# Weight sums of a seven-product matmul scheme: two by one accumulating DMA each, two on VectorE, with another order of the operands

## The chip, the cores and the metric

The kernel runs on one core of a Trainium2 chip. The metric is device time in microseconds (us), the median of several runs of the same program. The core has five engines that matter here: TensorE (PE; its weight loads are listed as PEld), VectorE (DVE), ScalarE (ACT), GpSimd (POOL) and SyncE (SP). SP issues most DMAs, POOL issues the DMAs that add to their destination while they write it.

## The reference

One step of a hybrid encoder layer for 512 prompt frames and 64 sample frames, 576 columns in all. Everything is float32.

```
h   = x @ W_in                            # combined projection for two groups of heads
mix = concat(ForgettingAttention(h_A), IndexedSparseAttention(h_B))
x   = LN1(alpha * x + mix @ W_o)
x   = LN2(alpha * x + relu(x @ W_up)^2 @ W_down)      # 1024 -> 4096 -> 1024
x   = x + sigmoid(x @ W_g + b_g) * (p @ W_ple)
```

The change touches only the line with `W_up` and `W_down`.

## The kernel before, in words

**Split weights.** TensorE multiplies in a rounded float32 format, so each weight tile is split into a high part (a cast on ACT, line 185, tile `whl` from `wraw` or `wsum`) and a low part (source minus high part on DVE, line 189), and each product is three matmuls: high times high, high times low, low times high. The activations are split in the same way.

**Groups and pairs.** `W_up` and `W_down` are cut into eight groups of 512 hidden units. Groups 0 and 1 are done directly. In groups 2 to 7 of `W_up`, and for groups 2 to 5 of `W_down`, two 128-column weight tiles form a *pair*, and the four 2 by 2 block products of a pair are made with seven products in place of eight. A pair needs seven operands, called P1, Z1, U2, P2, U3, X4, Z2. With b11, b21 the two halves of the first tile and b12, b22 those of the second, the program's sources are: P1 = b11, P2 = b21, Z2 = b22, and four sums: Z1 = b12 + b11, U3 = b12 + b22, U2 = b11 + b12 + b22, X4 = U2 + b21. There are 20 pairs: 12 of `W_up` and 8 of `W_down`, in the order 4 up, 4 down, 4 up, 4 down, 4 up.

**How a pair is loaded.** `Weights.load` takes two of four raw slots (`wraw`) as soon as every split of the pair that held them has been put into the program. SP loads the two tiles (line 159). `sum_loads` makes the sums in a tile `wsum` of two halves, t0 and t1 (two such tiles exist): SP loads b12 into t0 (line 221) and b11 into t1 (line 222); POOL adds b22 to t0 (line 223), adds b11 to the first half of the second raw tile, which is then Z1 (line 224), and adds t0 to t1, which is then U2 (line 225). Line 209, the function `total`, makes X4 on DVE from t1 and b21, into b11's place.

**What sets the order.** Each operand has a number `h`, in the order in which TensorE uses it (in `W_up` pairs that of `range(7)`, in `W_down` pairs that of the list `D_SEQ`, which goes by names). The two split instructions and `total` wait in a list sorted by a key near `h`. `drive` steps the main generator; one step (tick) is six matmuls, a product of a pair has 12 matmuls, so a pair of `W_up` is 14 ticks. At each tick `WT.step(2)` puts up to two pieces into the program, the first of the list only, and only if its due time (`when`, in ticks after the load) has come and if the ring of split tiles (`hl_ring`, nine in this stage) has room: `h - oldest < len(hl_ring)`. `WT.half` forces what is still missing when a product needs it. The framework then places the instructions on the engines by its own time estimates; the order in the program is the priority, not always the order on an engine. Each engine works its own list strictly in that order.

**Evacuation.** In `up_sums`, P1, U2 and U3 accumulate one after the other in one bank of a PSUM tile, P2 goes to its other bank, Z1 and Z2 accumulate in a second tile, X4 has a third. What is read between them: P1 and U2 copied to `u` by ACT (lines 1416, 1417), `r0 = P2 + u0` on DVE (line 1418), U3 copied by ACT and `r3 = Z - u0` on DVE (line 1419), then lines 1420 and 1421 for X4 and Z2. `r` and `u` are tiles of a pool; after Z2 the functions `after1` to `after3` square and split `r` (lines 1365 to 1392; lines 1375 and 1376 write the tiles `hq` and `hs`). In `down_sums` DVE adds each finished product to `Y` (line 1453). A done function is put into the program six matmuls after its product ends.

**Memory.** `WT.ring` gives split slots: six ("a"), three ("b") and, up to group 1 only, four more ("l").

Of the kernel before, what the change touches and what calls it, by code (L numbers as in the profile page):

```python
# [9 lines left out]
F32 = mybir.dt.float32  # L10
F32R = mybir.dt.float32r
AF = mybir.ActivationFunctionType
OP = mybir.AluOpType
# [19 lines left out]
HW = NT // 2  # L33
# [3 lines left out]
def tile_hybrid_step(ctx: ExitStack, tc: tile.TileContext, I, O):  # L37
    nc = tc.nc
    PE, ACT, DVE, POOL, SP = nc.tensor, nc.scalar, nc.vector, nc.gpsimd, nc.sync
# [4 lines left out]
    def f(ap):  # L44
        return ap.bitcast(F32)
# [13 lines left out]
    evq, clock = [], [0]  # L59
# [38 lines left out]
    LOADT = 4  # L98
# [16 lines left out]
    class Weights:  # L115
# [21 lines left out]
        def load(self, issue=True, force=False):  # L137

            if self.loaded == len(self.items):
                return False  # L140
            it = self.items[self.loaded]
            if len(it["aps"]) == 2 and self.sums is None:
                assert not force
                return False
            slots = sorted(self.raw_ring, key=lambda x: self.raw_own.get(x[1], -1))[:len(it["aps"])]
            for _, tag in slots:
                prev = self.raw_own.get(tag, -1)
                while prev >= 0 and self.items[prev]["left"]:
                    if not force:
                        return False  # L150
                    self.emit()
            views = []
            for (pool, tag), ap in zip(slots, it["aps"]):
                self.raw_own[tag] = self.loaded
                k, c = ap.shape[1:]
                t = pool.tile([128, 1024], F32, name="wraw", tag=tag)
                v = t[:, :k * c].rearrange("p (k c) -> p k c", k=k)
                if issue:
                    SP.dma_start(v, ap)
                views.append(v)  # L160
            if len(it["aps"]) == 2:
                self.sum_loads(views, it["aps"])
            self.raw[self.loaded] = views
            it["when"] = {h: clock[0] + LOADT * len(it["aps"]) for h in it["h"]}
            if len(it["aps"]) == 2:
                for x, n in zip((Z1, U2, U3, X4), (3, 4, 3, 4)):
                    it["when"][it["h"][x]] = clock[0] + LOADT * n
            ps = self.pieces_of(it, views)
            it["left"] = len(ps)
            for key, h, fn in ps:  # L170
                self.np += 1
                insort(self.pieces, (key, self.np, it, h, fn))
            self.loaded += 1
            return True
# [18 lines left out]
        def pieces_of(self, it, views):  # L193

            eng = POOL if it["pool"] else DVE
            k, c = views[0].shape[1:]
            if len(it["h"]) == 2:
                if k == 1:
                    cuts = [views[0][:, :, :c // 2], views[0][:, :, c // 2:]]
                else:  # L200
                    cuts = [views[0][:, :(k + 1) // 2], views[0][:, (k + 1) // 2:]]
                hs = [self.split(h, src, eng) for h, src in zip(it["h"], cuts)]
                return [(h + 1.5 * x, h, fns[x]) for h, fns in zip(it["h"], hs) for x in (0, 1)]
            b11, b21, b12, b22 = [v[:, x:x + 4] for v in views[:2] for x in (0, 4)]
            tot = views[2]
            h = it["h"]

            def total():
                DVE.tensor_tensor(b11, tot[:, 1], b21, OP.add)
            ps = [(max(h[P1] + 1.6, h[X4] - 1.4), h[X4], total)]  # L210

            for x, src in ((P1, b11), (Z1, b12), (U2, tot[:, 1]), (P2, b21), (U3, tot[:, 0]), (X4, b11), (Z2, b22)):
                high, low = self.split(h[x], src, DVE)
                ps += [(h[x], h[x], high), (h[x] + 1.5, h[x], low)]
            return ps

        def sum_loads(self, views, aps):

            t = self.sums()
            b11, b21, b12, b22 = [ap[:, x:x + 4] for ap in aps for x in (0, 4)]  # L220
            SP.dma_start(t[:, 0], b12)
            SP.dma_start(t[:, 1], b11)
            POOL.dma_start(t[:, 0], b22, accum_op=OP.add)
            POOL.dma_start(views[1][:, 0:4], b11, accum_op=OP.add)
            POOL.dma_start(t[:, 1], t[:, 0], accum_op=OP.add)
            views.append(t)

        def landed(self):
# [45 lines left out]
            return Unit([self.hv[h] for h in it["h"]], k, c)  # L274


    P1, Z1, U2, P2, U3, X4, Z2 = range(7)
    WT = Weights()

    def gemm(ps, W, kmap, aH, aL, cols, yield_every=6, first=True, last=True, wc=slice(0, 128), k0=0,  # L280
# [772 lines left out]
    for x, tag in ((0, "k32"), (1, "t2")):  # L1053
        t = sb.tile([128, NT], F32, name="praw", tag=tag)
# [33 lines left out]
    fb = ctx.enter_context(tc.tile_pool(name="fb", bufs=1))  # L1088
    psN = ctx.enter_context(tc.tile_pool(name="psN", bufs=1, space=PS))
    psB = ctx.enter_context(tc.tile_pool(name="psB", bufs=1, space=PS))  # L1090
    WT.ring(fb, 1, 3, "b")
    pS = ExitStack()
    fs = pS.enter_context(tc.tile_pool(name="fs", bufs=1))
    pL = ExitStack()
# [213 lines left out]
    def sums_of_x():  # L1308

        q = {(h, k): Y[:, 4 * k:4 * k + 4, (A, B)[h]] for h in (0, 1) for k in (0, 1)}  # L1310
        s12 = base.tile([128, 2, 2, 4, HW], F32R, name="s12", tag="AH")
        SX[1], SX[2] = [[s12[:, x, part] for part in (0, 1)] for x in (0, 1)]
        s3 = fs.tile([128, 2, 4, HW], F32R, name="s3")
        SX[3] = [s3[:, part] for part in (0, 1)]
        SX[4] = [t[:, 0:4, B] for t in (BH, BL)]
        r1, r2 = [fs.tile([128, 4, HW], F32, name="r", bufs=2) for _ in range(2)]

        def split(x, r):
            ACT.copy(SX[x][0], r)
            yield 1  # L1320
            DVE.tensor_tensor(SX[x][1], r, f(SX[x][0]), OP.subtract)
            yield 1

        DVE.tensor_tensor(r1, q[1, 0], q[1, 1], OP.subtract)
        yield 1
        yield 1
        DVE.tensor_tensor(r2, r1, q[0, 0], OP.subtract)
        yield 1
        yield from split(1, r1)
        yield from split(2, r2)  # L1330
        DVE.tensor_tensor(r1, q[0, 0], q[1, 0], OP.subtract)
        yield 1
        DVE.tensor_tensor(r2, q[0, 1], r2, OP.add)
        yield 1
        yield from split(3, r1)
        yield from split(4, r2)
# [12 lines left out]
    def up_sums(g, quarters=False):  # L1349
# [7 lines left out]
        def pair(m):  # L1357
            hs = WT.items[U["P", g, m]]["h"]

            r = fs.tile([128, 4, HW], F32, name="r", bufs=2)  # L1360
            u = fs.tile([128, 2, HW], F32, name="u")
            tt = DVE.tensor_tensor

# [49 lines left out]
            ps = {P1: G[:, 0, :HW], P2: G[:, 1, :HW], Z1: Z}  # L1413
# [19 lines left out]
        for m in range(2):  # L1433
            yield from pair(m)
# [71 lines left out]
    drive(seq(wo2(B, L1B, 0), ple()), 24, L1, 24, False)  # L1506
    drive(up(0, (L1A, L1B)), 16, L1, 16, False)
    XS = sums_of_x()
    n_xs = 11

# [163 lines left out]
```

## Time and profile before

| | |
|---|---|
| median of 3 runs | 840.4 us (839.18 to 842.44) |
| the profiled execution | 842.88 us, its span 841.2 us |
| PE busy | 799.1 us (95% of the span), 5820 matmuls |
| PEld busy | 770.3 us (92%) |
| DVE busy | 566.3 us (67%) |
| ACT busy | 478.1 us (57%) |
| POOL busy | 183.6 us (22%) |
| DMA | 107.70 MB, mean 128 GB/s |

A share is that of the whole span; a stage can look different. The stage with the pairs lies between about 440 and 735 us. "Idle before" in a row is the time the engine stood still ahead of that instruction, with what ended it behind the arrow. PEclk is the share of full speed that the clock of TensorE was granted. Buffer numbers are left out of tile names: `s` stands for the sums of x, `hs` and `hq` for those of the hidden units, `g`, `n` and `m` for PSUM tiles.

### The profile page before, as it was taken

Reading aid. Unit: us, or ns where it says so; the run is one execution under the profiler, and the core shown is the slowest. Engines: PE = TensorE matmul, PEld = TensorE weight load, DVE = VectorE, ACT = ScalarE, POOL = GpSimd, SP = SyncE. Lnnn points to the kernel's source line nnn. Section 1 sums busy time; section 2 is a strip of 40 time slices with the busy share of each in tenths; the row PEclk is TensorE's granted clock in tenths of the full one; section 3 lists DMA queues with packets and bytes.
Section 4 is the critical chain, followed back from the end, with each engine's and each line's share of the span. In section 5 each row is a group of like instructions: output and inputs, shape, how many; then the busy total and the mean of one; then the engine's idle time right before and its main releaser. Section 6 shows DMA issues by size and latency. Waiting matters only on the chain.

```text
span 841.2 us, 15352 instructions
## 1 busy us (share of the span) xinstructions
PE 799.1 (95%) x5820; PEld 770.3 (92%) x5820; DVE 566.3 (67%) x1188; ACT 478.1 (57%) x1041; POOL 183.6 (22%) x191
## 2 busy tenths in 40 slices
PE   7999899999999999999999889989889899999997
PEld 7998898899999999999999788988889799899997
DVE  5789999955458557897444567666668556567643
ACT  5578555788888544785312457335665237635451
POOL 7203435354531101200002111222112120012200
PEclk9999999999999999999999899999989999999999
DMA  8435333163213224323136757877667774741011
GB/s 283 159 59 139 93 93 107 66 199 110 85 55 104 67 97 151 135 104 126 52 74 164 161 139 175 199 173 197 160 141 190 183 184 119 261 153 51 14 38 64
DMA packets 44618, 107.70 MB, mean 128 GB/s; under 512 B 6656, under 2 KB 10496, under 8 KB 44416
## 3 DMA queue, kind: packets, MB, share of 16 engines
q1 hardware_dynamic: 35904, 90.98, 34.5%
q0 software_dynamic: 8640, 15.73, 11.7%
q8 instruction: 46, 0.75, 0.4%
q14 instruction: 28, 0.23, 0.1%
HBM read 87.36 MB, written 9.54 MB: 115 GB/s over the span
## 4 chain that ended last, share of the span: by engine, by line
PE 58%; DVE 14%; DMA 11%; issue 10%; ACT 5%; POOL 1%; SPq 0%; DVEq 0%; POOLq 0%; ACTq 0%
PE g L287 33%; PE m L287 11%; PE n L287 4%; DMA wsum<-wsum 3%; DMA wsum<-in_w_down_dram 2%; DVE dbias L655 2%; DMA wsum<-in_w_up_dram 2%; DVE m L653 2%; ACT whl L185 2%; DMA wraw<-in_w_up_dram 2%; DVE whl L189 1%; DMA wraw<-in_w_down_dram 1%; PE V L930 1%; PE T L56 1%; DVE PT L911 1%
## 5 line engine op out<-in xcount | busy, mean ns | idle before, releaser
L185 ACT CAST whl<-wraw 128x512 fp32r<-128x512 f32 (+1 forms) x234 | 140.3, 612 | 158.5 <-PE g L287 120.7
L189 DVE TENSOR_TENSOR whl<-wraw,whl 128x512 fp32r<-128x512 f32 (+1 forms) x200 | 138.6, 705 | 87.4 <-ACT whl L185 86.6
L287 PE MATMUL g<-BH,whl 128*128 128x288 f32 (+2 forms) x864 | 184.5, 299 | 0.3 <-ACT u L1419 0.2
L287 PE MATMUL m<-AH,whl 128*128 128x288 f32 x736 | 178.7, 310 | 0.0
L287 PEld LDWEIGHTS g<-BH,whl 128*128 128x128 f32 x864 | 143.1, 190 | 3.2 <-ACT u L1419 1.1
L287 PEld LDWEIGHTS m<-AH,whl 128*128 128x128 f32 x736 | 127.4, 190 | 1.1
L287 PE MATMUL g<-BL,whl 128*128 128x288 f32 (+2 forms) x432 | 128.0, 297 | 0.0
L287 PE MATMUL m<-AL,whl 128*128 128x288 f32 x368 | 109.6, 298 | 0.0
L287 PEld LDWEIGHTS g<-BL,whl 128*128 128x128 f32 x432 | 82.0, 190 | 0.1
L287 PEld LDWEIGHTS m<-AL,whl 128*128 128x128 f32 x368 | 70.1, 191 | 0.1
L862 ACT ACTIVATE sP<-sP,st 128x128 f32<-128x128 f32 (+4 forms) x72 | 39.7, 551 | 36.5 <-DVE st L854 36.2
L189 POOL TENSOR_TENSOR whl<-wraw,whl 128x512 fp32r<-128x512 f32 x34 | 44.5, 1307 | 62.5 <-ACT whl L185 50.8
L287 PE MATMUL g<-s,whl 128*128 128x288 f32 x288 | 46.5, 304 | 10.3 <-DVE r L1418 9.7
L287 PE MATMUL g<-hidE,whl 128*128 128x288 f32 (+2 forms) x384 | 52.9, 295 | 1.0 <-ACT u L1419 1.0
L287 PEld LDWEIGHTS g<-hidE,whl 128*128 128x128 f32 x384 | 51.5, 188 | 1.3 <-ACT u L1419 1.2
L287 PEld LDWEIGHTS g<-s,whl 128*128 128x128 f32 x288 | 40.3, 191 | 13.3 <-DVE r L1418 11.7
L287 PE MATMUL g<-hidO,whl 128*128 128x288 f32 (+2 forms) x384 | 52.2, 296 | 0.0
L185 ACT CAST whl<-wsum 128x512 fp32r<-128x512 f32 x40 | 24.8, 619 | 47.2 <-PE g L287 20.5
L287 PEld LDWEIGHTS g<-hidO,whl 128*128 128x128 f32 x384 | 51.4, 189 | 0.0
L287 PE MATMUL g<-hq,whl 128*128 128x288 f32 x288 | 47.2, 303 | 1.9 <-ACT u L1419 1.0
L911 DVE TENSOR_TENSOR PT<-T,PT 128x128 fp32r<-128x128 f32 (+1 forms) x64 | 31.0, 485 | 22.0 <-ACT PT L910 21.7
L287 PEld LDWEIGHTS g<-hq,whl 128*128 128x128 f32 x288 | 40.6, 190 | 4.8 <-ACT u L1419 1.4
(301 smaller groups left out, 1649.1 us busy)
## 6 DMA issues: line engine op xcount, KB each, us to landing
wraw<-in_w_up_dram SPq DMA_DIRECT2D x32, 512.0 KB, 4.4
wraw<-in_w_down_dram SPq DMA_DIRECT2D x32, 512.0 KB, 4.3
wraw<-in_w_qkv_dram SPq DMA_DIRECT2D x23, 512.0 KB, 4.1
wsum<-in_w_up_dram SPq DMA_DIRECT2D x24, 256.0 KB, 4.1
wsum<-wsum POOLq DMA_DIRECT2D x20, 256.0 KB, 4.9
wsum<-in_w_down_dram SPq DMA_DIRECT2D x16, 256.0 KB, 4.1
wraw<-in_w_gate_dram SPq DMA_DIRECT2D x8, 512.0 KB, 4.4
wraw<-in_w_o_dram SPq DMA_DIRECT2D x8, 384.0 KB, 3.1
```

What stands on the lines that cost most here:

```text
L56: PE.transpose(out, in_, ident[:n, :n])
L185: ACT.copy(self.hv[h][0], src)
L189: eng.tensor_tensor(lv, src, f(hv), OP.subtract)
L287: PE.matmul(ps, W(w, kw, wc), a[:, ka, cols], start=(first and i == 0), stop=(last and i == n - 1), skip_group_check=chain)
L653: DVE.max(m, s)
L655: DVE.match_replace(out=s, in_to_replace=m, in_values=s, imm_value=GONE)
L862: ACT.activation(j["P"], j["P"], AF.Exp, bias=j["st"][:, 0:1], scale=-1.0, accum_out=s)
L911: DVE.tensor_tensor(t[:, 1, :n, c], v, f(t[:, 0, :n, c]), OP.subtract)
L930: PE.matmul(ps[:, c], w, j["PT"][:, x, kb, c], start=(kb == 0 and x == 0), stop=(kb == i and x == 1))
```

## The change

U2 is no longer made by two more DMAs (SP's load of b11 into t1 and POOL's addition of t0 to t1) but by an addition on DVE, `t1 = t0 + b11`, a new piece in the sorted list with the key `h[U2] - 0.4`. Z1 and U3 stay as one accumulating DMA each; X4 stays on DVE. The due times become 10 ticks for P1, P2 and Z2 and 18 ticks for the four sums, where they were 8 for P1, P2 and Z2, 12 for Z1 and U3, and 16 for U2 and X4; for single tiles they stay at 4. The order of the operands in `W_up` pairs becomes P1, P2, U2, Z1, U3, X4, Z2; that of `W_down` pairs, by names, stays. The ring "b" has four split slots in place of three; the tile `r` has one buffer in place of two, and the second tile of `sums_of_x` shares the place of `hsum`.

```
-            it["when"] = {h: clock[0] + LOADT * len(it["aps"]) for h in it["h"]}
+            it["when"] = {h: clock[0] + LOADT for h in it["h"]}
             if len(it["aps"]) == 2:
-                for x, n in zip((Z1, U2, U3, X4), (3, 4, 3, 4)):
-                    it["when"][it["h"][x]] = clock[0] + LOADT * n
+                for x in range(7):
+                    it["when"][it["h"][x]] = clock[0] + (10 if x in (P1, P2, Z2) else 18)
...
-            def total():
-                DVE.tensor_tensor(b11, tot[:, 1], b21, OP.add)
-            ps = [(max(h[P1] + 1.6, h[X4] - 1.4), h[X4], total)]
+            ps = [(h[U2] - 0.4, h[U2], lambda: DVE.tensor_tensor(tot[:, 1], tot[:, 0], b11, OP.add)),
+                  (max(h[P1] + 1.6, h[X4] - 1.4), h[X4], lambda: DVE.tensor_tensor(b11, tot[:, 1], b21, OP.add))]
...
             SP.dma_start(t[:, 0], b12)
-            SP.dma_start(t[:, 1], b11)
             POOL.dma_start(t[:, 0], b22, accum_op=OP.add)
             POOL.dma_start(views[1][:, 0:4], b11, accum_op=OP.add)
-            POOL.dma_start(t[:, 1], t[:, 0], accum_op=OP.add)
...
-    P1, Z1, U2, P2, U3, X4, Z2 = range(7)
+    P1, P2, U2, Z1, U3, X4, Z2 = range(7)
...
-    WT.ring(fb, 1, 3, "b")
+    WT.ring(fb, 1, 4, "b")
...
-        r1, r2 = [fs.tile([128, 4, HW], F32, name="r", bufs=2) for _ in range(2)]
+        r1, r2 = [fs.tile([128, 4, HW], F32, name=n) for n in ("r", "hsum")]
...
-            r = fs.tile([128, 4, HW], F32, name="r", bufs=2)
+            r = fs.tile([128, 4, HW], F32, name="r")
```

## The prediction

> **What bounds the kernel now.** I read the page first, then the waits of TensorE in the stage with the pairs, then the rows around its longest waits, and last what each of those waited for.
>
> ```profile
> span 841.2 us, 15352 instructions
> PE 799.1 (95%) x5820; PEld 770.3 (92%) x5820; DVE 566.3 (67%) x1188; ACT 478.1 (57%) x1041; POOL 183.6 (22%) x191
> PEclk9999999999999999999999899999989999999999
> ...
> 440.00:735.00 295.00, 269.77 (x1866) 257.73 (x1865) 186.98 (x347) 148.93 (x284) 50.08 (x58) 0.96 0.70 174
> ...
> PE g L287 <- DVE r L1418: 9.7, 5, 4.8
> PE g L287 <- DVE Y L1453: 6.8, 4, 3.8
> PE n L287 <- DVE r L1419: 4.9, 3, 4.0
> ```
>
> TensorE is the bound, yet in the 295 us with the pairs it stands still for 25.2 us (295 less 269.77), at a clock of 0.96. The reader is to see that it never waits there for a weight's DMA: the three largest lines are all evacuations by DVE. Here are the five long ones (start, duration, idle before in brackets), and one short one:
>
> ```profile
> 475.00 0.61 PE L287 MATMUL n<-BH,whl 128*128 128x288 f32 x1 [3.98 <-DVE r L1419]
> 503.63 1.07 PE L287 MATMUL g<-s,whl 128*128 128x288 f32 x6 [3.01 <-DVE r L1418]
> 517.58 1.06 PE L287 MATMUL g<-s,whl 128*128 128x288 f32 x6 [0.88 <-DVE r L1418]
> 548.92 1.33 PE L287 MATMUL g<-hs,whl 128*128 128x288 f32 x5 [2.69 <-DVE Y L1453]
> 611.58 1.81 PE L287 MATMUL g<-s,whl 128*128 128x288 f32 x6 [4.79 <-DVE r L1418]
> 658.92 3.13 PE L287 MATMUL g<-hs,whl 128*128 128x288 f32 x12 [3.79 <-DVE Y L1453]
> ```
>
> The five make 18.26 us. Each also costs clock: the windows behind them (length; busy PE, PEld, DVE, ACT, POOL; granted clock; DMA share; GB/s), and one behind the short wait:
>
> ```profile
> 475.00:481.00 6.00, 6.00 (x25) 6.00 (x26) 4.03 (x9) 4.26 (x10) 1.44 (x2) 0.51 0.64 132
> 503.60:508.10 4.50, 4.25 (x20) 3.90 (x21) 2.60 (x5) 3.06 (x7) 0.50 (x1) 0.63 0.77 163
> 548.90:553.10 4.20, 4.18 (x20) 4.20 (x21) 2.52 (x5) 0.62 (x1) 1.42 (x2) 0.59 0.97 223
> 611.60:616.60 5.00, 4.95 (x19) 4.60 (x20) 2.55 (x5) 2.96 (x7) 0.85 (x1) 0.50 0.85 166
> 658.90:663.00 4.10, 4.08 (x21) 4.10 (x22) 2.31 (x5) 0.62 (x1) 0.98 (x2) 0.65 0.89 208
> 517.00:527.00 10.00, 8.28 (x54) 7.30 (x55) 7.39 (x17) 8.29 (x17) 0.87 (x1) 1.00 0.65 175
> ```
>
> Length times one minus clock is 2.94, 1.67, 1.72, 2.50 and 1.44 us, 10.27 in all; the wait of 0.88 us cost none. So 28.5 us hang on five moments. Why DVE was late there is in its own rows and ACT's:
>
> ```profile
> 473.89 0.69 DVE L209 TENSOR_TENSOR wraw<-wsum,wraw 128x512 f32<-128x512 f32 x1 [4.32 <-DMA wsum<-wsum]
> 546.75 0.69 DVE L209 TENSOR_TENSOR wraw<-wsum,wraw 128x512 f32<-128x512 f32 x1 [4.29 <-DMA wsum<-wsum]
> 656.75 0.69 DVE L209 TENSOR_TENSOR wraw<-wsum,wraw 128x512 f32<-128x512 f32 x1 [5.38 <-DMA wsum<-wsum]
> 501.26 1.14 ACT L185 CAST whl<-wraw 128x512 fp32r<-128x512 f32 x2 [3.35 <-DMA wraw<-in_w_down_dram]
> 609.22 1.14 ACT L185 CAST whl<-wraw 128x512 fp32r<-128x512 f32 x2 [5.13 <-DMA wraw<-in_w_down_dram]
> ```
>
> In three, `total` (line 209) stood at the head of DVE's list until line 225's DMA had landed, with the evacuation behind it. In two, ACT stood at a cast whose source line 224 adds to, and DVE behind ACT.
>
> **The change part by part.** *The chain of U2.* The DMAs of POOL around these moments, and two rows of the page (KB each, median us to landing):
>
> ```profile
> 468.36 0.85 POOL L225 DMA_DIRECT2D wsum<-wsum  x1 [5.11 <-DMA wsum<-in_w_up_dram]
> 495.57 0.86 POOL L225 DMA_DIRECT2D wsum<-wsum  x1 [6.20 <-DMA wraw<-in_w_down_dram]
> 496.20 1.10 POOL L224 DMA_DIRECT2D wraw<-in_w_down_dram  x1
> 602.92 1.14 POOL L224 DMA_DIRECT2D wraw<-in_w_down_dram  x1
> ...
> wsum<-wsum POOLq DMA_DIRECT2D x20, 256.0 KB, 4.9
> wsum<-in_w_up_dram POOLq DMA_DIRECT2D x12, 256.0 KB, 5.1
> ```
>
> Line 225 goes out when t0 has landed, so at 468.36 both inputs of the new DVE addition were there, 5.5 us before `total` could start at 473.89. Two additions of 0.69 us end at about 469.8; the wait of 4.32 us is gone, and so are, by the same reckoning (4.9 us median against 4.29 and 5.38), the other two to within half a microsecond. Term A: 3.98 + 2.69 + 3.79 = 10.46 us of standing still, and their clock, 2.94 + 1.72 + 1.44 = 6.10. What is late next there is t0 itself, which the next term but one prices.
>
> *The addition for Z1.* Line 224 stands behind line 225 on POOL (496.20 behind 495.57) and now goes out right behind line 223. It took 501.26 less 496.20 = 5.06 us and 609.22 less 602.92 = 6.30 us, with line 225's bytes moving beside it. Line 222 and 225 move 256 KB each; at the stage's 174 GB/s 256 KB are 1.5 us. I take 0.6 us earlier issue and 1.5 us from lighter traffic, and for the longer one 1 us more: of 3.01 and 4.79 us, 0.9 and 1.7 remain. Term B: 5.2 us. For the clock I take all of 1.67 and half of 2.50, 2.9 us, as the remaining waits are near the 0.88 that cost none. The bounds: nothing saved (both raw tiles land no sooner, and their landing released line 225) and all, 7.80 + 4.17.
>
> [...]
>
> *The added DVE work.* Twenty additions of 0.69 us are 13.8 us on an engine busy 187 of 295 us; by themselves they lie beside TensorE's work. Their danger is the wait for t0, at the head of DVE's list. The nearest rows are line 225's, which show when t0 had landed, and the cast of U2 of the same pair:
>
> ```profile
> 475.47 0.85 POOL L225 DMA_DIRECT2D wsum<-wsum  x1 [4.61 <-DMA wsum<-in_w_up_dram]
> 483.77 0.62 ACT L185 CAST whl<-wsum 128x512 fp32r<-128x512 f32 x1 [0.76 <-PE g L287]
> ```
>
> The cast came 8.3 us after t0 and waited for a free slot, not for data. If the addition stands just ahead of its cast, it waits for nothing; if it is placed as early as its inputs allow, it can wait. Bounds: 0, and what `total` costs TensorE now, 10.46 us. I take 2.0, nearer to the row of no wait.
>
> *The order and the single `r`.* P2 is now second, so line 1418 comes two products sooner, just behind the last reads of the previous pair's `r`:
>
> ```profile
> 492.30 0.46 DVE L1421 TENSOR_TENSOR r<-n,u 128x288 f32<-128x288 f32 x1 [0.25 <-PE n L287]
> 495.41 0.75 DVE L1376 TENSOR_TENSOR hq<-r,hq 128x576 fp32r<-128x576 f32 x1
> 494.88 1.81 PE L287 MATMUL g<-s,whl 128*128 128x288 f32 x12
> ```
>
> `r` is free at 496.16 and line 1418 (0.45 us) done at 496.6. A product takes some 1.6 us (12 matmuls, pipelined), so P1, P2 and the first half of U2 end 4.0 us after Z2 at 492.1, at 496.1; the second half waits for line 1418, as the row at 503.63 shows for U3 now: 0.5 us at each of the six places where a `W_up` pair that feeds `hq` follows another, 3.0 us. Bounds: 0 (PE takes other matmuls first) and two splits of 0.69 us queued ahead, 1.9 x 6 = 11. Z1, now fourth, gains 3.2 us of slack, worth nothing where it isn't late; in `W_down`, where it was, the order stays.
>
> *Due times, ring, memory.* A pair's load goes out some 14 ticks before the ring has room for its P1 and 18 before U2, so 10 and 18 hardly bind: nothing. One more slot lets splits run one product (1.6 us) further ahead; since both load and split move, nothing. SP loses 20 issues, POOL 20 of 0.86 us and their waits; neither is waited for otherwise. `hsum` in `sums_of_x` is free before its first pair: nothing.
>
> *New places.* Every engine's order is laid anew. I add one new wait of the smallest kind that costs clock: 2.69 + 1.72 = 4.4 us, between none and two.
>
> *Sum:* 10.46 + 6.10 + 5.2 + 2.9 - 2.0 - 3.0 - 4.4 = 15.3 us less. The profiled execution took 842.88 us (1.68 outside the span), 2.48 above the median of 840.4; the changed one's would be 827.6, the median 825.1. I predict 825.
>
> **The rivals.**
>
> *The new addition blocks DVE (slower).* DVE works its list in order, and the addition needs no free slot, only t0 and b11; placed as early as its inputs seem ready, it stands there for w us in each of 20 pairs. TensorE paid 10.46 us for 13.99 us of `total`'s three long waits, 0.75 for one, so 15w. Without the 2.0 the gains are 17.3 us; it decides from w = 1.2 us. At 1.7 us the cost is 25.5 and the time 840.4 - 17.3 + 25.5 = about 849. For it: three of `total`'s waits were over 4 us, so the order on DVE does count on DMAs sooner than they land. Against it: the chain ahead is one DMA shorter, and the cast at 483.77. Chance 0.15.
>
> *Eaten at the pair boundaries (no change).* Term B saves nothing, line 1418 costs its upper 11.2: 10.46 + 6.10 - 2.0 - 11.2 - 4.4 = 1 us less, 839. For it: DVE's and ACT's work behind Z2 is densest there. Chance 0.13.
>
> *The DMAs for Z1 stay late.* Only A: 16.56 - 2.0 - 3.0 - 4.4 = 7.2 less, 833. For it: at 495.57 the raw tile's landing was the release. Chance 0.10.
>
> *All five vanish and nothing new comes:* 28.5 less, 812. For it: waits this short have one cause each. Chance 0.12.
>
> *The due times do nothing* (above) is part of my forecast.
>
> The forecast has the other 0.50, with 816 to 832 as its own range (the addition, the order and new waits at 0; or one wait more and the addition at twice its price). A change under 0.5% (4.2 us) can hardly be told from none. Faster: 0.50 + 0.10 + 0.12 = 0.72; same 0.13; slower 0.15. The range 812 to 843 leaves out the slower rival and little else.
>
> **What would show it.** Right: line 209's additions no longer waiting for `wsum` over 2 us, at most one row of PE with over 2 us of idle time between 440 and 735, a clock of 0.98 to 0.99 there, a DMA share of about 0.6, and 17 us of PE's idle time (25.2 - 10.46 - 5.2 + 2.0 + 3.0 + 2.69). Wrong: DVE waiting for `wsum` at the new addition in most pairs (first rival); PE waiting for line 1418 or 1416 behind each Z2 (second); ACT still at `wraw` near the first `W_down` pair (third); or a wait in a stage before 440, where I expect no change.

## The result and the profile after

The changed kernel takes 835.02 us (median of 8 runs, 832.27 to 836.41) against 842.1 for the kernel before, run beside it: a ratio of 0.9909, interval 0.9883 to 0.9934. It is faster by 7 us. The forecast was 15.3 us.

Line numbers behind 209 are three lower now: `total` is still line 209, the new addition on DVE line 208, POOL's addition of b22 to t0 line 221 and that for Z1 line 222, the matmul line 284, the copies of P1 and U2 lines 1413 and 1414, `r0` line 1415, `r3` line 1416, the addition to `Y` line 1450.

First the page of the changed kernel:

```profile
span 834.7 us, 15261 instructions
PE 794.7 (95%) x5820; PEld 765.5 (92%) x5820; DVE 577.4 (69%) x1208; ACT 478.1 (57%) x1041; POOL 166.8 (20%) x171
PEclk9999999999999999999999999999999999999999
```

No slice shows a lower clock any more. Now the same stage of 295 us as before, and four stretches behind waits of TensorE (columns as in the prediction):

```profile
440.00:735.00 295.00, 272.33 (x1920) 259.58 (x1919) 201.00 (x373) 154.29 (x293) 30.90 (x36) 0.98 0.52 136
540.00:545.00 5.00, 4.71 (x24) 4.71 (x25) 3.55 (x7) 0.62 (x1) 0.00 (x0) 0.67 0.29 67
571.00:577.00 6.00, 5.70 (x31) 5.70 (x32) 1.79 (x4) 1.82 (x4) 0.88 (x2) 0.72 0.69 179
649.00:654.00 5.00, 4.73 (x34) 4.55 (x35) 3.44 (x7) 0.62 (x1) 0.00 (x0) 1.00 0.18 56
664.00:669.00 5.00, 5.00 (x26) 5.00 (x27) 3.16 (x6) 0.62 (x1) 0.00 (x0) 0.66 0.14 52
```

The clock rose from 0.96 to 0.98, but TensorE still stands still for 22.7 us (295 less 272.33; 25.2 before). In the waits of that stage line 209 has no wait for a DMA any more; the addition ahead of it has (total, times, longest):

```profile
DVE wsum L208 <- DMA wsum<-in_w_up_dram: 23.5, 8, 4.5
...
PE g L284 <- DVE Y L1450: 7.5, 5, 2.7
...
PE g L284 <- ACT u L1413: 6.0, 4, 2.3
...
PE g L284 <- DVE r L1415: 5.3, 3, 2.4
DVE wsum L208 <- DMA wraw<-in_w_up_dram: 4.8, 2, 3.4
```

The two lines of L208 are 28.3 us in ten pairs. Two pairs stand before 440, and one of `W_down` waited 0.9 us: over the whole run DVE stood at the new addition for 35.6 us in 13 of the 20 pairs, among them all twelve of `W_up`, which is 1.8 us for a pair on average. And these are the rows: PE's with over 1.4 us of idle time ahead of them, and the waiting additions on DVE that stand before them.

```profile
470.58 0.68 DVE L209 TENSOR_TENSOR wraw<-wsum,wraw 128x512 f32<-128x512 f32 x1
474.08 0.69 DVE L208 TENSOR_TENSOR wsum<-wsum,wraw 128x512 f32<-128x512 f32 x1 [2.81 <-DMA wsum<-in_w_up_dram]
477.79 1.06 PE L284 MATMUL g<-s,whl 128*128 128x288 f32 x6 [2.34 <-ACT u L1413]
507.91 1.06 PE L284 MATMUL g<-s,whl 128*128 128x288 f32 x6 [1.48 <-DVE r L1415]
538.82 0.69 DVE L208 TENSOR_TENSOR wsum<-wsum,wraw 128x512 f32<-128x512 f32 x1 [2.69 <-DMA wsum<-in_w_up_dram]
540.29 2.14 PE L284 MATMUL g<-hs,whl 128*128 128x288 f32 x12 [1.76 <-DVE Y L1450]
559.62 0.84 POOL L221 DMA_DIRECT2D wsum<-in_w_up_dram  x1 [10.44 <-DMA wsum<-in_w_up_dram]
566.70 0.69 DVE L208 TENSOR_TENSOR wsum<-wsum,wraw 128x512 f32<-128x512 f32 x1 [4.27 <-DMA wsum<-in_w_up_dram]
570.80 0.45 DVE L1415 TENSOR_TENSOR r<-g,u 128x288 f32<-128x288 f32 x1
571.30 1.06 PE L284 MATMUL g<-s,whl 128*128 128x288 f32 x6 [2.37 <-DVE r L1415]
616.05 1.06 PE L284 MATMUL g<-s,whl 128*128 128x288 f32 x6 [1.48 <-DVE r L1415]
647.79 0.69 DVE L208 TENSOR_TENSOR wsum<-wsum,wraw 128x512 f32<-128x512 f32 x1 [3.54 <-DMA wsum<-in_w_up_dram]
649.27 1.86 PE L284 MATMUL g<-hs,whl 128*128 128x288 f32 x12 [2.60 <-DVE Y L1450]
662.43 0.69 DVE L208 TENSOR_TENSOR wsum<-wsum,wraw 128x512 f32<-128x512 f32 x1 [3.43 <-DMA wraw<-in_w_up_dram]
664.00 2.77 PE L284 MATMUL g<-hs,whl 128*128 128x288 f32 x12 [2.72 <-DVE Y L1450]
689.15 0.69 DVE L208 TENSOR_TENSOR wsum<-wsum,wraw 128x512 f32<-128x512 f32 x1 [2.52 <-DMA wsum<-in_w_up_dram]
692.35 0.40 PE L284 MATMUL g<-BH,whl 128*128 128x288 f32 x1 [2.08 <-ACT u L1413]
```

Read one moment: at 559.62 POOL issues the addition to t0, at 566.70 DVE's new addition can start after 4.27 us of waiting, six more instructions of DVE's list follow, line 1415 comes at 570.80, and TensorE goes on at 571.30 after 2.37 us of standing still. The waiting moved from `total` to the new addition, an instruction that stands earlier in the same list. In the rows at 477.79 and 692.35 the way goes over ACT: before it could copy P1 it had waited 2.78 and 2.03 us for DVE's lines 1381 and 1418, which stand behind the addition.

The two rows of 1.48 us lie where the waits at 503.63 and 611.58 were, but have another cause: ACT no longer waits there for the raw tile that line 222 adds to; ahead of line 1415 DVE still works on the pair before and reads its `r` until 506.82 (the rows at 615.55 are the same):

```profile
ACT whl L185 <- DMA wraw<-in_w_down_dram: 0.4, 1, 0.4
...
506.07 0.75 DVE L1373 TENSOR_TENSOR hq<-r,hq 128x576 fp32r<-128x576 f32 x1
506.74 0.75 DVE L1373 TENSOR_TENSOR hs<-hsum,hs 128x576 fp32r<-128x576 f32 x1
507.41 0.45 DVE L1415 TENSOR_TENSOR r<-g,u 128x288 f32<-128x288 f32 x1
```

### The profile page after: what moved, and what is told of

Read it like the earlier page. It is cut to its first block, busy times and chain, and to the rows that moved or that the text cites. A ratio compares the mean times of both kernels' runs of the same rounds, so it can differ in the third digit from the quotient of the medians.

```text
span 834.7 us, 15261 instructions
## 1 busy us (share of the span) xinstructions
PE 794.7 (95%) x5820; PEld 765.5 (92%) x5820; DVE 577.4 (69%) x1208; ACT 478.1 (57%) x1041; POOL 166.8 (20%) x171
## 5 line engine op out<-in xcount | busy, mean ns | idle before, releaser
L284 PE MATMUL g<-BH,whl 128*128 128x288 f32 (+2 forms) x864 | 181.0, 297 | 3.2 <-ACT u L1413 2.1
L284 PEld LDWEIGHTS g<-BH,whl 128*128 128x128 f32 x864 | 141.1, 188 | 5.0 <-ACT u L1413 2.9
L284 PE MATMUL m<-BH,whl 128*128 128x288 f32 x192 | 43.6, 304 | 0.0
```

The lines of the kernel that those rows point to most:

```text
L284: PE.matmul(ps, W(w, kw, wc), a[:, ka, cols], start=(first and i == 0), stop=(last and i == n - 1), skip_group_check=chain)
```

## The experiments

Each was timed beside the kernel before, which took 840.8 to 843.2 us in the five sets of runs. Differences between two of the changed kernels are of medians; by the ratios the 12.9 us of the first experiment are 10.1, those of the old order 17.7, 10.4 and 6.8 in place of 12.9, 11.7 and 6.5, and the others shift by less than 1 us. The expectations number their theories: 1 is that the new addition loses time by waiting on DVE for t0, 3 that it loses it by its work there, 5 that the new order gains of itself; the others are said in words where they occur.

**The addition on POOL.** POOL waits for its own DMA, DVE only gets the sum later.

```
-  lambda: DVE.tensor_tensor(tot[:, 1], tot[:, 0], b11, OP.add)
+  lambda: POOL.tensor_tensor(tot[:, 1], tot[:, 0], b11, OP.add)
```

> The changed kernel with one edit: the addition t1 = t0 + b11 runs on POOL in place of DVE. Theory 1 (the new addition stands at the head of DVE's list until t0 has landed: 24.8 us of such waits between 440 and 735, behind which PE stood 15.9 us and lost 5.0 us of clock): these waits leave DVE, the time falls from 835 to 814 to 822 us, and PE's waits on lines 1413, 1415 and 1450 shrink to under 8 us together. Rival 2 (the waits of PE come from the new order of the operands and the single r): 835 within 3 us. Rival 3 (13.8 us more work on DVE is what costs): 825 to 832 us. What can spoil it: POOL's addition takes longer (a split of this size takes it 1.3 us) and keeps POOL's own DMAs waiting.

Measured 822.11 us, ratio 0.9789 (0.9756 to 0.9821), 12.9 us below the changed kernel. Theory 1 gave 814 to 822, just missed. In the stage PE's clock is 1.00, DVE waits for no weight's DMA, and POOL stands at the addition for 32.4 us in 9 pairs until t0 of `W_up` has landed. This changes wait and work at once, so the next two were to part them.

**The addition on POOL, an idle one on DVE.** The first try at the work alone: an addition of b21 to itself in the old place, its result unused.

```
+  (h[U2] - 0.4, h[U2], lambda: DVE.tensor_tensor(fh.tile([128, 4, 128], F32, name="idle"), b21, b21, OP.add)),
```

> As the kernel with the addition on POOL, and DVE does 20 additions of the same size of b21 with itself into a tile that nobody reads, so DVE has the work of the changed kernel without the wait for t0. Theory 1: within 4 us of the kernel with the addition on POOL. Rival 3 (work on DVE): back near 835 us. Rival 2: 835 within 3 us, as the other.

Measured 830.11 us, ratio 0.9890 (0.9851 to 0.9928): 8 us slower than without it. It fits neither theory, and a line of its waits says why it settles nothing:

```profile
DVE idle L208 <- DMA wraw<-in_w_up_dram: 9.0, 8, 2.5
```

The idle addition itself waited for the raw tile that it reads, 9.0 us in 8 pairs. It brought a wait along with the work.

**The addition on POOL, idle work that waits for nothing.** Twenty additions of 0.68 us on DVE (13.6 us), reading the high part of P1, which lies in the split ring.

```
+  def idle_add():
+      v = f(self.hv[h[P1]][0])
+      DVE.tensor_tensor(fh.tile([128, 4, 128], F32, name="idle"), v, v, OP.add)
+  ps.append((h[P1] + 1.55, h[P1], idle_add))
```

> The kernel with the addition on POOL, and 20 additions of the same size on DVE that read the high part of P1 right behind P1's low split, so they wait for nothing that DVE did not wait for already; the result is read by nobody. It prices the 13.8 us of DVE work alone. Theory 1: 822 to 825 us. Rival 3: 828 to 832 us, as the idle additions that had to wait for a raw tile (830).

Measured 823.92 us, ratio 0.9784 (0.9743 to 0.9825), against 0.9789 without that work. Work of the same length, placed where it waits for nothing (the trace shows no idle time of DVE ahead of it), costs nothing that can be told; theory 3, which had 828 to 832, falls.

**t1 in a tile of its own, with one buffer.** The addition stays on DVE and does the same work.

```
...
-  WT.sums = lambda: fh.tile([128, 2, 4, 128], F32, name="wsum", bufs=2)
+  WT.sums = lambda: (fh.tile([128, 1, 4, 128], F32, name="wsum", bufs=2), fh.tile([128, 1, 4, 128], F32, name="usum", bufs=1))
```

> The changed kernel with t1 in a tile of its own with one buffer, the addition still on DVE. The addition then also needs the previous pair's split of U2 and its X4 done, so it is placed later on DVE and t0 has more time to land. Theory 1 (the wait for t0 at the head of DVE's list is the cost): DVE's waits at the addition fall from 28 us to under 12 us in the stage and the time from 835 to between 820 and 829 us. Rival 3 (the work on DVE is the cost): 835 within 3 us, the work is the same.

Measured 817.15 us, ratio 0.9704 (0.9671 to 0.9737), below the 820 to 829 that theory 1 gave. The stage:

```profile
440.00:735.00 295.00, 286.20 (x2062) 273.42 (x2061) 214.19 (x391) 159.82 (x303) 33.49 (x39) 1.00 0.55 148
```

Of its waits the greatest of DVE for a weight's DMA and the greatest of PE:

```profile
DVE usum L208 <- DMA wraw<-in_w_down_dram: 4.5, 2, 2.4
...
PE g L284 <- DVE r L1415: 3.0, 2, 1.5
```

And DVE around the addition:

```profile
470.34 0.68 DVE L209 TENSOR_TENSOR wraw<-usum,wraw 128x512 f32<-128x512 f32 x1
471.42 0.46 DVE L1418 TENSOR_TENSOR r<-n,u 128x288 f32<-128x288 f32 x1 [0.40 <-PE n L284]
...
473.26 0.68 DVE L189 TENSOR_TENSOR whl<-usum,whl 128x512 fp32r<-128x512 f32 x1
...
477.44 0.45 DVE L1415 TENSOR_TENSOR r<-g,u 128x288 f32<-128x288 f32 x1
...
478.41 0.68 DVE L208 TENSOR_TENSOR usum<-wsum,wraw 128x512 f32<-128x512 f32 x1
```

In the changed kernel the addition of this pair stood at 474.08, the next instruction after `total` and ahead of line 1418, and waited 2.81 us. Here it can't: the one buffer of t1 is still to be read by the low part of U2 of the pair before, at 473.26. It stands behind that, line 1418, the splits of the hidden units and line 1415, at 478.41, and waits for nothing. From the issue of t0's accumulating DMA to the moment when DVE stands at the addition it is now 7.0 us (median of the twelve pairs of `W_up`), 3.8 in the changed kernel. Same engine, same work, another place in the list: 17.9 us.

**The old order of the operands.** Three pairs of kernels that differ in the order alone: the changed kernel, the one with the addition on POOL, the one with t1 alone in a tile.

```
-  P1, P2, U2, Z1, U3, X4, Z2 = range(7)
+  P1, Z1, U2, P2, U3, X4, Z2 = range(7)
```

> The changed kernel with the old order of the seven operands (P1, Z1, U2, P2, U3, X4, Z2), all else as changed. Theory 1: 835 within 4 us, since DVE still waits for t0 at the addition, about 25 us in the stage. Rival 2 (order and single r): about 822 to 828 us, with PE's waits on lines 1413 and 1415 (5.3 and 6.0 us in the changed kernel) gone.

> The kernel with the addition on POOL, with the old order of the seven operands. With the addition on DVE the old order cost 13 us (848 against 835). Theory 4 (the order matters by where DVE's waits hit, TensorE's wait on r3 = Z - u0 or a shorter one): without those waits it matters little, 819 to 826 us. Rival 5 (the new order is worth about 13 us by itself, as it gives Z1 more time): 832 to 838 us.

> The kernel with t1 in a tile of its own with one buffer (817 us), in the old order of the operands. Rival 5 (the new order is worth about 12 us by itself): 826 to 833 us. Theory 4 (the order matters only by where DVE's waits for t0 hit, and those are gone here): 815 to 821 us.

Measured 847.93, 833.76 and 823.63 us, ratios 1.0119 (1.0067 to 1.0172), 0.9912 (0.9877 to 0.9947) and 0.9785 (0.9733 to 0.9837); with the new order 835.02, 822.11 and 817.15. The new order gains 12.9, 11.7 and 6.5 us. The first result fits none of the theories, the second theory 5, the third lies between the two that were named. Two lines of the waits of the first (changed kernel, old order), and the longest wait of TensorE in the third (t1 alone, old order):

```profile
DVE wsum L208 <- DMA wsum<-in_w_up_dram: 29.5, 8, 4.6
...
PE n L284 <- DVE r L1416: 12.5, 4, 4.4
```

```profile
503.50 2.96 PE L284 MATMUL g<-s,whl 128*128 128x288 f32 x12 [3.58 <-ACT u L1413]
```

That the order gains, also where DVE waits for no sum, is shown: theory 5 had it so. Why is not: the waits that the old order brings have other names from kernel to kernel (line 1416, `r3`, in the first; the copy of line 1413 in the third). In the first pair the old order also makes DVE wait longer at the addition, 36.6 us in the stage against 29.2; in the other two pairs that can't be it.

**The swap alone.** The kernel before, with line 222's and line 225's DMA taken out and the addition put in; order, ring, `r` and due times as before. Then the same with `POOL` for `DVE` in the added line.

```
-  SP.dma_start(t[:, 1], b11)
...
-  POOL.dma_start(t[:, 1], t[:, 0], accum_op=OP.add)
...
+  (h[U2] - 0.4, h[U2], lambda: DVE.tensor_tensor(tot[:, 1], tot[:, 0], b11, OP.add)),
```

> The kernel before with only the swap: line 222's load and line 225's addition by DMA go, the addition t1 = t0 + b11 comes to DVE; due times, order, ring and r as before. Theory 1: the swap alone brings both the gain (the waits of 18.3 us and their clock of 10.3 us) and the new waits, so 832 to 839 us. Rival 2: 822 to 828 us, the gain without the cost of the order.

> The kernel before with only the swap, and the addition on POOL: old order, three ring slots, two r. The kernel with the addition on POOL, four slots and one r had 834 us in the old order and 822 in the new. If the old order is what costs those 12 us (rival 5): 830 to 838 us. If it costs only together with the single r or the larger ring (theory 7): 820 to 827 us.

On DVE 839.91 us, ratio 0.9985 (0.9953 to 1.0016): no change, 0.9 us above theory 1's range. On POOL 829.37 us, 0.9847 (0.9793 to 0.9901), between the two theories and telling them apart badly. By itself the swap gives back what it gains; DVE's additions wait 37.3 us there (19.2, 14.9 and 3.2 in the waits). With the wait on POOL the gain is 13 us.

**The old due times.**

```
+  it["when"] = {h: clock[0] + LOADT * len(it["aps"]) for h in it["h"]}
...
+      for x, n in zip((Z1, U2, U3, X4), (3, 4, 3, 4)):
+          it["when"][it["h"][x]] = clock[0] + LOADT * n
```

> The changed kernel with the due times of before (8 ticks for P1, P2, Z2; 12 for Z1 and U3; 16 for U2 and X4). The prediction's step (they hardly bind): 835 within 3 us. Rival: the later due times keep splits out of the way of evacuations, 838 to 845 us without them.

Measured 833.49 us, ratio 0.9916 (0.9879 to 0.9954), beside the 0.9909 of the changed kernel. The due times do nothing.

**Three split slots and two `r`.** In the changed kernel, and in the one with t1 alone.

```
-  WT.ring(fb, 1, 4, "b")
+  WT.ring(fb, 1, 3, "b")
...
-  r = fs.tile([128, 4, HW], F32, name="r")
+  r = fs.tile([128, 4, HW], F32, name="r", bufs=2)
```

> The changed kernel with the memory of before: three slots in ring b and two buffers of r. The prediction's step (a single r keeps line 1418 waiting at six places, 3 us in all, up to 11; the ring slot is worth nothing): 824 to 833 us. Rival 6 (the slot of the ring is worth more than the second r): 837 to 845 us.

> The kernel with t1 in a tile of its own with one buffer (817 us), with three ring slots and two r. The prediction's step (3 us, up to 11, lost to the single r): 806 to 815 us. Rival 6 (the slot is worth more): 819 to 827 us. Rival 8 (neither matters): 815 to 819 us.

Measured 820.68 us, ratio 0.9747 (0.9698 to 0.9795), and 809.32 us, ratio 0.9608 (0.9552 to 0.9664). The first is below what was expected. The second is the fastest of all: 33 us below the kernel before in the same runs (842.67), and 3.1% below the changed one (809.32 / 835.02). Its stage, and the two greatest lines of its PE's waits:

```profile
440.00:735.00 295.00, 290.73 (x2114) 280.40 (x2113) 217.93 (x398) 161.99 (x308) 38.14 (x42) 1.00 0.57 153
```

```profile
PE g L284 <- DVE Y L1450: 3.0, 2, 1.6
...
PE g L284 <- DVE r L1415: 1.2, 1, 1.2
```

**Three split slots, the single `r` kept.** No run has four slots and two `r` together; slot and `r` were parted this way round, in the same two kernels.

```
-  WT.ring(fb, 1, 4, "b")
+  WT.ring(fb, 1, 3, "b")
```

> The changed kernel with three split slots, and still a single r; nothing else differs. With two r and three slots it took 820.7 us, as changed 835.0. Theory (the single r carries the 14.3 us, since line 1415 must wait for the last splits of the previous pair's r): 833 to 838, the slot is worth nothing. Rival (the fourth slot carries it, since it lets splits run further ahead and stand in front of evacuations): 820 to 826. Between 827 and 832 both share it.

> The kernel with t1 in a tile of its own, single-buffered (817.2 us with four slots and one r, 809.3 with three slots and two r), now with three slots and one r. Theory (the single r carries the 7.8 us): 815 to 819. Rival (the fourth slot): 808 to 812.

Measured 822.53 us, ratio 0.9759 (0.9714 to 0.9805), and 814.51 us, ratio 0.9671 (0.9617 to 0.9725). In the changed kernel the rival holds: the fourth slot costs 12.5 us of the 14.3, the single `r` 1.8, less than the intervals tell apart. With t1 alone the result lies between the theory and the rival: the slot is worth 2.7 us and the `r` 5.2, and by the intervals neither can be told from nothing. The first kernel's stage, its greatest waits of DVE for t0 and of PE, and the one long wait that is left:

```profile
440.00:735.00 295.00, 281.76 (x2025) 269.88 (x2024) 210.20 (x386) 156.71 (x297) 35.20 (x40) 0.99 0.56 150
```

```profile
DVE wsum L208 <- DMA wsum<-in_w_up_dram: 15.0, 5, 6.1
PE g L284 <- DVE r L1415: 7.2, 5, 4.6
```

```profile
464.24 0.69 DVE L208 TENSOR_TENSOR wsum<-wsum,wraw 128x512 f32<-128x512 f32 x1 [6.11 <-DMA wsum<-in_w_up_dram]
469.03 1.81 PE L284 MATMUL g<-s,whl 128*128 128x288 f32 x6 [4.59 <-DVE r L1415]
```

With a slot less DVE comes to the addition later: 5.5 us after the issue of t0's DMA in the median pair of `W_up`, 3.8 with the slot. Its waits for `W_up`'s t0 are 15.0 us in 5 pairs, 23.5 in 8 with the slot (all its waits in the stage 19.2 and 29.2), and TensorE stands still for 13.2 us (295 less 281.76) in place of 22.7.

## Why the prediction was right and wrong

*Right: what hung on the chain of U2.* Line 209 waits for no DMA, and the three waits of TensorE behind it are gone: 10.46 us and 6.10 of clock, as forecast.

*Right, and larger than forecast: the addition for Z1.* ACT's waits of 3.35 and 5.13 us for the raw tile are gone, so all of the 7.80 us of TensorE behind them went. In the 4.5 us from 507.90 and the 5 us from 616.00 the clock is 1.00, so all 4.17 us of clock came back too. Together 12.0, the upper bound, against 8.1.

*Right: due times and DVE's work at nothing.* Shown by the old due times (833.49) and by the idle work (823.92 against 822.11).

*Wrong: the added addition, taken at 2.0 us.* The six rows of PE above with 1.76 to 2.72 us stand behind a waiting line 208 each; they make 13.87 us, and three of them clock: 5 x 0.33 + 6 x 0.28 + 5 x 0.34 = 5.0 us. That is 18.9 us; the waits alone are above the prediction's upper bound of 10.46. The tally closes: 16.56 + 12.0 less 2.96 (order and `r`, below) and 18.9 is 6.7 us, and the span fell by 6.5. The experiments price the same thing by taking the wait off DVE (12.9 us) or by another place in its list (17.9 us). The step that failed is the reading of the cast at 483.77, 8.3 us after t0: a cast needs a free slot to write to, the addition does not, and the trace has it right behind `total` of the pair before (470.58, then 474.08). The first rival had this in words and was given 0.15. Its mean wait came (1.7 us for a pair, 1.8 measured), its price did not: it took 0.75 us of TensorE's time for one of DVE's wait, and the 18.9 us for 35.6, clock included, are 0.53. With that and the 8.3 us of gains beyond the forecast (below) the kernel ended faster, where the rival had it slower.

That DVE holds to the order of its list, the trace shows: at 566.70 DVE had stood for 4.27 us, and line 1415, which needed nothing of the sum, came behind it at 570.80. The description of the kernel says the same of every engine; the argument needs it of DVE alone.

*Wrong: the ring at nothing.* "Since both load and split move, nothing" left out that the room in the ring, `h - oldest < len(hl_ring)`, holds back every piece of the list, the addition too. The load moves too, but the traces show that the addition gains on it: with four slots DVE stands there 3.8 us after the issue of t0's DMA, with three 5.5. The fourth slot cost 12.5 us in the changed kernel; where the addition's wait is gone (t1 alone) only 2.7. So it seems for the most part the same loss as the last, seen from its other side, and the two don't add: 17.9 for the one, 12.5 for the other, 20.5 for both (835.02 less 814.51).

*Right in the wait, wrong in sign as a whole: order and single `r` at 3.0 us of loss.* The wait that the term describes is there: line 1415 behind the last reads of the previous pair's `r`, two rows of 1.48 us, 2.96 in all, at two places in place of six. (With the addition on POOL it is 5.7 us in eight rows.) With t1 alone the same two rows are 1.48 us long with four slots and one `r`, 0.54 with three slots, and gone with the second `r`. But the term held only what the order costs. In three pairs of kernels it gains 6.5 to 12.9 us on the whole, which was nowhere in the sum; the reason stays open.

*New places, 4.4 us:* none over 1.4 us came beside the waits named above. So the size failed, not the direction: 16.9 us more were lost at the addition than the 2.0, and 8.3 us went better than forecast (3.9 at Z1, 4.4 not lost in new places), which makes the 8.6 us between 15.3 and the 6.7 of the tally. What the order gains and the slot costs are differences between kernels; the tally holds them only as waits.

Of the rivals' figures one is added up wrongly: in the second, 10.46 + 6.10 - 2.0 - 11.2 - 4.4 is 1 us more time, 841.4, not 1 us less. And that the third rival's 833 lies nearest to the result is chance: it kept the DMAs for Z1 late, and they were not.

Of what was to be seen: line 209 without waits and the clock of 0.98 came; a single row of PE over 2 us (there are five), 17 us of standing still (22.7) and a DMA share of 0.6 (0.52) did not. The sign named for the first rival came: DVE waited at the new addition in 13 of 20 pairs. Open stays why the new order gains, and whether the 2.7 and 5.2 us of slot and `r` in the fastest kernel are more than their intervals.

## What to carry to other kernels

When a DMA's sum is replaced by an instruction on an engine that works in order, as DVE does here, the wait can move to that instruction, here 35.6 us in 13 of the 20 pairs: what counts is its place in the list against the landing of its input, not its 0.69 us of work. Price it from when the input lands to when the instruction can stand first, and don't read its place off a later consumer that is held back by something else. Depth of a ring of buffers is a place too: one slot more let a waiting instruction in earlier (3.8 us after the issue of t0's DMA in place of 5.5) and cost 12.5 us here; try such a trade apart from the change that it comes with.

## What was not expected of the hardware

The clock did not follow the length of the wait here. After 1.76 us (540.29) it was 0.67 and after 2.37 us (571.30) 0.72, while after 2.60 us (649.27) it stayed at 1.00. The trace records the granted clock with its times: between 440 and 735 us it was 0.50 for three whole stretches of 3.41 us, from 541.66, 572.38 and 664.54, which lie 9 and 27 such stretches apart, and 1.00 otherwise. Cut into stretches of that length, in step with those three, the trace shows most of the difference:

```profile
538.25:541.66 3.41, 1.65 (x13) 1.41 (x12) 2.84 (x6) 0.62 (x1) 0.00 (x0) 1.00 0.33 59
541.66:545.07 3.41, 3.41 (x16) 3.41 (x15) 1.89 (x4) 0.62 (x1) 0.00 (x0) 0.50 0.41 94
...
644.06:647.47 3.41, 2.61 (x20) 2.37 (x18) 0.19 (x1) 1.78 (x3) 0.20 (x1) 1.00 0.95 149
647.47:650.89 3.42, 1.62 (x12) 1.63 (x13) 3.10 (x7) 0.00 (x0) 0.00 (x0) 1.00 0.11 19
650.89:654.30 3.41, 3.41 (x26) 3.23 (x25) 1.55 (x3) 0.85 (x2) 0.00 (x0) 1.00 0.28 89
```

Each of the three came behind a stretch of the same grid with 1.76, 2.34 and 2.72 us of standing still. The wait of 2.60 us fell on two stretches, with 0.80 and 1.80 us, and cost no clock. In the sixteen traces of this case, between 400 and 760 us, each of the 25 stretches at full clock with more than 1.82 us of standing still was followed by one at 0.50, and none with less than 1.46; of the 22 in between, six were. So in these traces the loss went with how much of one stretch stood still, which the length of a wait alone does not tell; what parts the 22 was not shown. A stretch at 0.50 is 1.7 us lost, half of 3.41.

The accumulating DMA of 256 KB (line 221) took from 559.62 to 566.70, 7.1 us, before DVE could start, where the prediction went by medians of 4.9 to 5.1.
